# Attention tiles in a pool that closes among the gate tiles, and maxima spread one tile later, in a two-layer decoder trunk

## The chip, the core and the metric

One core of one Trainium2 chip runs the whole program. Its engines are TensorE (PE in the profile; PEld is its weight load), VectorE (DVE), ScalarE (ACT), GpSimd (POOL) and SyncE (SP), whose queue issues the DMAs. Each engine works through its own instructions in the order in which they were queued, and waits on semaphores. The metric is device microseconds of one execution: lower is better. Shown runs of the kernel before have a median of 1673.81 us.

## The reference, cut to what matters

Two post-norm layers over 1024 tokens of 1024 channels. Layer A mixes with dilated sliding-window attention (three groups of keys, merged by their softmax sums), layer B with a sliding window and learned sinks. Both multiply the mixer's output by a SiLU gate before the output projection:

```python
o = einsum('gbsh,gbshd->bshd', softmax(lses), outs)       # layer A: three groups merged
z = h[..., -A_WIDTH:]                                      # gate, from the same input projection
mix = (o * silu(z)) @ w_out
x = layer_norm(ALPHA * x + mix, ln_g[i], ln_b[i])
x = x + sigmoid(x @ ple_w_gate[i]) * (p[i] @ ple_w_proj[i])
```

Everything is float32; the kernel makes it from float16 halves (below).

## The kernel before

**Products.** Every operand of a projection is scaled by a power of two and split into a float16 high part and a low part; a product is three float16 matmuls (high times high, high times low, low times high; L270 to L272). A *tile* of a projection is 128 tokens by 512 output columns: 24 matmuls, with one PSUM buffer of the three that the pool `ps_lin` has, until another engine has read it out.

**Weights.** Weights come in blocks of 1024 rows by 512 columns (`Block`). Each needs its four loads (L102), four reductions of the largest magnitude (L108), the maximum's spreading over all partitions, and four splits on ScalarE and VectorE (L131, L132). The spreading has two halves: `max_diag` makes a diagonal matrix on VectorE (`mdd`, L228), and `max_spread` multiplies it by ones on TensorE (L235), so that VectorE can reduce the result to the scale. All of this is one generator, `weight_steps`, of ten steps for each block. After each tile `prepare(n)` adds n to a credit and takes that many steps: 1.6 for most tiles, 5 for gate tiles of the second half (L934), 2 for output tiles, 3 for tiles of the last product. A step that cannot go on yet (the slot of the block before last is still read, or the pool it needs is not open) yields False and the credit falls to 0. `next_block` takes all steps that are left of a block that is needed now. Two raw buffers, two slots `whl`, and one slot each of `wo` (in the pool `pw`) and `wg` (in the pool of that name) hold the blocks.

**Order.** The program is written out tile by tile; what is written earlier has the higher priority, and a list scheduler, with an estimate of all durations, puts the instructions on the engines' queues in the order in which it finds them ready. So an instruction can be queued well ahead of its place in the program, and the order on each queue is fixed when the program runs.

**Layer A.** 18 blocks of V and of Q and K, eight tiles each. Behind the tiles run the attention *units*: scores (L383), maxima, exponentials, a transposing DMA `pT<-phl` (L402), and values (L414 to L416), queued with a lag. `work_done` counts tiles; `later` and `sub_tick` let units come due by it. The last units of layer A still run beside the first gate tiles. For each 128 tokens and half of the heads, a `merge` joins the three groups (tiles `gt`, loads L745, store L767), one stage for each tile. Then come the gate tiles: 16 of them, eight for each half of the columns (`z_block`, `z_tile`), whose rows `za` (`zb` in layer B) are stored to memory (L725).

**From gate to output projection.** `z_block` does the eight tiles of the first half and one of the second; `drain` then writes out what is left of units and merges, the pool `att` closes, and the pools `tp` (transposed rows) and `pw` (rows, `wo`, and the tables `g_b`, `b_b` of the norm) open over its space, on the other side of the free memory. A tile in a new pool waits until all that lay at its place is done. `mixed` then writes the seven other gate tiles; behind the fifth to the eighth tile of that half stands `rows(n)`: two loads (L894, L895), the product of mixer and gate on GpSimd (L898), the largest sum on ScalarE (L900), a split (L261, L262) and a transposing DMA `ogT<-rhl` (L874). Output tiles need `ogT`; `norm(n)` does two of them, then the norm, with `g_b` at L924. The pool `wg` opens behind the fourth output tile, when the pools below have closed. Layer B goes the same way, with its own pools `kv` and `att2`, and without merges; its units end in a store `ob<-mu` (L860).

## Time and profile before

| | us |
|---|---|
| three runs | 1684.5, 1673.64, 1673.81 |
| median | 1673.81 |
| the profiled execution | 1672.76 |
| its span, first to last instruction | 1670.9 |

The granted clock has a mean of 0.985 over the span; 1.0 stands for 2.4 GHz and 0.5 for 1.2 GHz. Times of rows are microseconds from the span's start. From the trace, the parts of the program lie as follows: gate tiles of layer A up to 1054.6, its output projection from 1064.9 to 1162.4, its last product to 1245.3, layer B's attention to about 1425 with its gate tiles beside and behind it to 1495.4, layer B's output projection to 1583.6.

### The profile page before, as it was taken

How to read it: one execution, taken by the hardware profiler on the slowest of the kernel's cores; microseconds unless marked ns; L12 is line 12 of the kernel's file. 1: busy time of each engine (PE TensorE's matmuls, PEld its weight loads, DVE VectorE, ACT ScalarE, POOL GpSimd, SP SyncE). 2: the span in 40 equal slices, each digit the busy share in tenths (PEclk: the TensorE clock that was granted, in tenths of full speed). 3: DMA queues.
4: the chain of work that ended last, by engine and by line, in shares of the span. 5: the costliest groups of instructions: out<-in, count | busy, mean ns of one | idle time of the engine just before them, and what ended most of it. 6: DMA issues, size and time to landing. Idle time of an engine off the chain costs nothing.

```text
span 1670.9 us, 29003 instructions
## 1 busy us (share of the span) xinstructions
PE 1587.2 (95%) x10579; PEld 879.7 (53%) x10579; DVE 1080.0 (65%) x2617; ACT 922.0 (55%) x2050; POOL 671.6 (40%) x481
## 2 busy tenths in 40 slices
PE   9899999999999889999999997789999999999999
PEld 3455666654555446666545543334456555544444
DVE  6756655655656875456556567788437989777731
ACT  4536755674775377556647844433333888854221
POOL 0205623532554665144235743343323452225441
PEclk9999999999999999999999998899999999999999
DMA  9617765774788777467648885989976798988963
GB/s 364 244 60 171 169 146 133 165 162 112 164 163 208 208 161 160 120 153 158 153 117 176 181 248 192 314 233 237 247 190 138 143 209 176 189 300 218 256 199 111
DMA packets 543791, 311.02 MB, mean 186 GB/s; under 512 B 473120, under 2 KB 494240, under 8 KB 543392
## 3 DMA queue, kind: packets, MB, share of 16 engines
q1 hardware_dynamic: 543648, 309.16, 73.6%
q8 instruction: 83, 1.36, 0.4%
q14 instruction: 60, 0.49, 0.1%
HBM read 137.78 MB, written 54.92 MB: 115 GB/s over the span
## 4 chain that ended last, share of the span: by engine, by line
PE 59%; DVE 14%; DMA 12%; issue 5%; POOL 4%; ACT 3%; SPq 2%; POOLq 0%; DVEq 0%; ACTq 0%
PE lin L270 18%; PE lin L272 18%; PE lin L271 18%; DMA pT<-phl 4%; DVE whl L132 3%; PE s L383 3%; DVE wpm L108 2%; DMA gt<-scr 2%; ACT sm L393 1%; DVE sm L387 1%; PE o L414 1%; PE o L416 1%; PE o L415 1%; POOL hl L356 1%; DMA wraw<-in_wg_dram 1%
## 5 line engine op out<-in xcount | busy, mean ns | idle before, releaser
L270 PE MATMUL lin<-whl,xhl 128*128 128x512 f16 x1280 | 488.9, 382 | 0.0
L271 PE MATMUL lin<-whl,xhl 128*128 128x512 f16 x1280 | 487.7, 381 | 0.0
L272 PE MATMUL lin<-whl,xhl 128*128 128x512 f16 x1280 | 487.5, 381 | 0.0
L399 POOL TENSOR_TENSOR phl<-sm,phl 128x1024 f16<-128x1024 f32 (+1 forms) x88 | 156.5, 1778 | 259.6 <-ACT phl L397 215.7
L349 POOL TENSOR_TENSOR t<-t,t 128x512 f32<-128x512 f32 (+1 forms) x120 | 152.2, 1268 | 232.1 <-DVE t L348 226.1
L272 PEld LDWEIGHTS <-xhl 128*128 128x128 f16 x1280 | 149.3, 117 | 125.8 <-issue 2.9
L270 PEld LDWEIGHTS <-xhl 128*128 128x128 f16 x1280 | 149.2, 117 | 117.4 <-issue 2.6
L108 DVE TENSOR_REDUCE wpm<-wraw 128x1 f32<-128x1024 f32 (+1 forms) x132 | 157.2, 1198 | 82.7 <-DMA wraw<-in_wa_dram 47.4
L271 PEld LDWEIGHTS <-xhl 128*128 128x128 f16 x1280 | 149.9, 117 | 115.2 <-issue 2.3
L393 ACT ACTIVATE sm<-sm,st,cs 128x128 f32<-128x128 f32 (+1 forms) x384 | 203.4, 531 | 3.3 <-ACT st L391 0.4
L356 POOL TENSOR_TENSOR hl<-t,hl 128x512 f16<-128x512 f32 (+1 forms) x120 | 142.7, 1189 | 136.0 <-ACT hl L355 136.0
L387 DVE CUSTOM_DVE_ANT_0 sm<-s,tab 128x256 f32<-128x256 f32 (+1 forms) x512 | 157.0, 359 | 53.7 <-PE s L383 51.9
L132 DVE SCALAR_TENSOR_TENSOR whl<-wraw,s,whl 128x1024 f16<-128x1024 f32 (+1 forms) x116 | 165.0, 1473 | 4.7 <-ACT whl L131 4.6
L345 DVE TENSOR_TENSOR t<-lin,rope 128x512 f32<-128x512 f32 (+1 forms) x120 | 78.9, 658 | 119.3 <-PE lin L272 83.1
L355 ACT ACTIVATE hl<-t 128x512 f16<-128x512 f32 (+1 forms) x120 | 72.1, 601 | 121.0 <-POOL t L349 119.2
L131 ACT ACTIVATE whl<-wraw,s 128x1024 f16<-128x1024 f32 (+1 forms) x116 | 121.9, 1122 | 12.6 <-DVE s L210 6.5
L272 PE MATMUL lin<-whl,x2T 128*128 128x512 f16 (+1 forms) x320 | 115.0, 359 | 0.0
L271 PE MATMUL lin<-whl,x2T 128*128 128x512 f16 (+1 forms) x320 | 115.0, 359 | 0.0
L270 PE MATMUL lin<-whl,x2T 128*128 128x512 f16 (+1 forms) x320 | 114.9, 359 | 0.0
L397 ACT ACTIVATE phl<-sm 128x1024 f16<-128x1024 f32 (+1 forms) x128 | 110.2, 861 | 2.7 <-DMA pT<-phl 1.5
L359 ACT ACTIVATE hl<-hl 128x512 f16<-128x512 f16 (+1 forms) x104 | 63.1, 607 | 59.0 <-POOL hl L356 58.8
L414 PEld LDWEIGHTS <-pT 128*128 128x128 f16 x800 | 72.2, 98 | 34.9 <-DMA pT<-phl 31.1
(190 smaller groups left out, 2901.7 us busy)
## 6 DMA issues: line engine op xcount, KB each, us to landing
wraw<-in_wa_dram SPq DMA_DIRECT2D x56, 512.0 KB, 5.2
scr<-st SPq DMA_DIRECT2D x96, 132.0 KB, 2.4
gt<-scr SPq DMA_DIRECT2D x48, 264.0 KB, 3.3
wraw<-in_wav_dram SPq DMA_DIRECT2D x24, 512.0 KB, 6.1
prh<-pro SPq DMA_DIRECT2D x32, 256.0 KB, 4.5
wraw<-in_wg_dram SPq DMA_DIRECT2D x16, 512.0 KB, 9.0
xg<-y SPq DMA_DIRECT2D x16, 512.0 KB, 3.7
wraw<-in_wb_dram SPq DMA_DIRECT2D x16, 512.0 KB, 6.3
```

The lines of the kernel that those rows point to most:

```text
L108: k.nc.vector.tensor_reduce(pm[:, c:c + 1], self.raw[:, c * q:(c + 1) * q], axis=AX.X, op=ALU.max, apply_absolute_value=True)
L131: nc.scalar.activation(hl[:, 0, sl], self.raw[:, sl], AF.Copy, scale=self.s)
L132: nc.vector.scalar_tensor_tensor(hl[:, 1, sl], self.raw[:, sl], self.s, hl[:, 0, sl], op0=ALU.mult, op1=ALU.subtract)
L270: mm(ps, xh(kt), wh, start=(kt == 0), stop=False)
L271: mm(ps, xh(kt), wl, start=False, stop=False)
L272: mm(ps, xl(kt), wh, start=False, stop=(kt == NK - 1))
L349: nc.gpsimd.tensor_add(t1[:, :nh * HD], t1[:, :nh * HD], t2[:, :nh * HD])
L356: nc.gpsimd.tensor_sub(hl[:, :nh, HD:P], rv, hl[:, :nh, 0:HD])
L387: nc.vector.tensor_tensor_reduce(sm[:, h, :nk], ps[:, i, :nk], mask, 1.0, -3e38, ALU.add, ALU.max, mx[:, h:h + 1])
L393: nc.scalar.activation(sm[:, h, :nk], sm[:, h, :nk], AF.Exp, bias=nbias[:, h:h + 1], scale=cs, accum_out=sums[:, h:h + 1])
L397: nc.scalar.activation(hl[:, 0], sm[:, :, :nk], AF.Copy)
L399: eng.tensor_sub(hl[:, 1], sm[:, :, :nk], hl[:, 0])
```

## The change

The pool `att` no longer holds the tiles of the merges, `st` and `gt`: they get a pool `attm` of their own, below it; the tile `hl` moves from `work` to `att`. The function `drain` is gone. The new `gate_tiles` writes all eight gate tiles of the first half, at three steps each, and as soon as no unit is due, queued or in the pipe, calls `leave`, which closes `att` (in layer B `att2` and `kv`) and opens `tp` and `pw`. `mixed` writes all eight tiles of the second half, at three steps each; merges go on beside them. When merges and gate tiles are written, `gate_pool` closes what is left below and opens the pool `wg`, now ahead of the output projection, and with `g_b` and `b_b` in it. In `Block.maxima` the step that spreads the maximum waits until 0.9 tiles more have been written since the diagonal, unless `next_block` is in a hurry (`rush`). At the start, four of the eleven last products of the per-layer inputs are written ahead of the first block's splits.

```diff
 UNIT_LAG = 1.67
 W_STEPS = 1.6
+SPREAD = 0.9
 W_OP = 2
 N_WAKE = 8
-Z_AHEAD = 1
+W_GATE = 3
...
         diag = k.max_diag(pm)
         yield True
+        at = k.work_done + SPREAD
+        while k.work_done < at and not k.rush:
+            yield False
         e = k.max_spread(diag)
...
-    def drain(self):
-        due, self.due = self.due, []
-        for e in due:
-            e[1]()
-        while self.units or any(self.pipe):
-            self.unit_step()
-        self.merge_every = 1
-        while self.merges or self.merging:
-            self.merge_step()
...
-        hl = w.tile([P, 12, P], F16, tag="hl", name="hl", bufs=3)
+        hl = self.att.tile([P, 12, P], F16, tag="hl", name="hl", bufs=3)
...
+                ple1(4)
                 while not self.blocks[0].done:
                     next(self.steps)
-                ple1(11)
+                ple1(7)
...
+        self.rush = True
         while not b.done:
             assert next(self.steps)
+        self.rush = False
...
         self.merge_every = 1
-        self.z_block(self.invx, lambda n: self.stat_a(0, n))
-        self.drain()
+        self.z_in = self.invx, lambda n: self.stat_a(0, n)
...
-    def z_block(self, invx, stat):
-
-        self.z_stat = stat
+    def z_block(self, half):
+
+        invx, self.z_stat = self.z_in
+        self.w_z = self.next_block()
+        self.cz = self.prod(invx, self.w_z.inv, 0.5, "cz")
+
+    def gate_tiles(self, leave):
+
         self.upt = 2.0
-        for half in range(2):
-            self.w_z = self.next_block()
-            self.cz = self.prod(invx, self.w_z.inv, 0.5, "cz")
-            for n in range(Z_AHEAD if half else NT):
-                self.z_tile(self.work, n, half)
-                self.progress()
-            if half == 0:
-                self.w_z.released = True
+        self.z_block(0)
+        for n in range(NT):
+            self.z_tile(self.work, n, 0)
+            self.progress(W_GATE)
+            if leave and not (self.due or self.units or any(self.pipe)):
+                leave()
+                leave = None
+        assert leave is None
+        self.w_z.released = True
...
-        g_b = pw.tile([P, D], F32, tag="g_b", name="g_b", bufs=1)
-        b_b = pw.tile([P, D], F32, tag="b_b", name="b_b", bufs=1)
-        nc.sync.dma_start(g_b, a["lng"][l].partition_broadcast(P))
-        nc.sync.dma_start(b_b, a["lnb"][l].partition_broadcast(P))
...
+        self.z_block(1)
         done = 0
-        for n in range(Z_AHEAD, NT):
+        for n in range(NT):
             self.z_tile(self.work, n, 1)
             self.tick()
-            self.prepare(5)
+            self.prepare(W_GATE)
             if n >= NT - ROWS_AHEAD:
                 rows(done)
                 done += 1
+        while self.merges or self.merging:
+            self.merge_step()
+        gp = gate_pool()
+        g_b = gp.tile([P, D], F32, tag="g_b", name="g_b", bufs=1)
+        b_b = gp.tile([P, D], F32, tag="b_b", name="b_b", bufs=1)
+        nc.sync.dma_start(g_b, a["lng"][l].partition_broadcast(P))
+        nc.sync.dma_start(b_b, a["lnb"][l].partition_broadcast(P))
         self.w_z.released = True
...
-            if n == 1:
-                wg = gate_pool()
...
-        with tc.tile_pool(name="att", bufs=2) as self.att:
-            self.layer_a()
-        tp, self.tp = opened("tp", 9, side="right")
-        pw, self.pw = opened("pw", 2, side="right")
+        for name in ("work", "attm"):
+            p, pool = opened(name, 2)
+            setattr(self, name, pool)
+            lower.append(p)
+        att, self.att = opened("att", 2)
+        self.layer_a()
+        pools = []
+
+        def row_pools(first, last):
+            for p in first:
+                close(p)
+            for name, bufs in last:
+                p, pool = opened(name, bufs, side="right")
+                setattr(self, name[:2], pool)
+                pools.append(p)
...
+        self.gate_tiles(lambda: row_pools([att], [("tp", 9), ("pw", 2)]))
...
+        self.gate_tiles(lambda: row_pools([att, kv], [("pw2", 2)]))
```

## Rows read from the trace of the kernel before

**Rows 1.** The page's first part: busy time, share, instructions.

```profile
PE 1587.2 (95%) x10579; PEld 879.7 (53%) x10579; DVE 1080.0 (65%) x2617; ACT 922.0 (55%) x2050; POOL 671.6 (40%) x481
```

**Rows 2.** TensorE's longest wait in total: us, times, longest one.

```profile
PE o L414 <- DMA pT<-phl: 23.4, 17, 2.8
```

**Rows 3.** Busy time by stretch: PE, PEld, DVE, ACT, POOL; clock, DMA share, GB/s.

```profile
951.00:1162.40 211.40, 179.98 (x943) 82.66 (x940) 162.73 (x332) 92.23 (x147) 96.23 (x59) 0.94 0.84 240
...
1017.00:1054.60 37.60, 28.85 (x122) 12.26 (x119) 24.80 (x50) 13.52 (x20) 12.45 (x11) 0.86 0.71 255
1054.60:1162.40 107.80, 88.50 (x388) 38.90 (x388) 90.74 (x181) 42.49 (x50) 45.98 (x26) 0.92 0.91 246
1162.40:1245.30 82.90, 82.90 (x386) 37.59 (x384) 36.27 (x46) 25.56 (x30) 23.33 (x18) 1.00 0.88 227
...
1495.40:1583.60 88.20, 84.63 (x385) 38.05 (x386) 67.22 (x128) 35.55 (x38) 38.25 (x22) 0.98 0.92 240
```

**Rows 4.** Timeline of TensorE at single instructions; in brackets the idle time before.

```profile
992.11 0.20 PE L414 MATMUL o<-vh,pT 128*128 128x64 f16 x1 [0.46 <-DMA pT<-phl]
...
1036.16 0.29 PE L235 MATMUL s<-mdd,ones 128*128 128x128 bf16 x1 [8.75 <-DVE mdd L228]
...
1064.86 0.58 PE L270 MATMUL lin<-whl,ogT 128*128 128x512 f16 x1 [10.23 <-ACT whl L131]
...
1498.97 0.26 PE L235 MATMUL s<-mdd,ones 128*128 128x128 bf16 x1 [3.62 <-DVE mdd L228]
```

**Rows 5.** Busy time by stretch around the idle times of layer A.

```profile
1027.40:1036.20 8.80, 0.05 (x2) 0.04 (x2) 8.73 (x20) 1.95 (x3) 3.63 (x3) 0.73 0.35 134
1036.20:1041.70 5.50, 5.50 (x14) 2.02 (x15) 2.58 (x4) 2.66 (x3) 0.00 (x0) 0.50 0.57 191
...
1054.60:1064.90 10.30, 0.07 (x2) 0.07 (x2) 10.23 (x19) 8.51 (x12) 4.86 (x3) 0.70 1.12 339
1064.90:1069.00 4.10, 4.10 (x10) 1.39 (x11) 4.10 (x5) 2.93 (x5) 2.63 (x2) 0.50 1.06 262
...
1114.00:1146.90 32.90, 24.12 (x98) 10.18 (x98) 28.69 (x64) 8.75 (x9) 14.11 (x8) 0.90 0.88 231
```

**Rows 6.** Timeline of the DMA issues on SyncE's queue, layer A.

```profile
1020.19 0.38 SPq L725 DMA_DIRECT2D za<-zu  x1
...
1036.73 0.37 SPq L767 DMA_DIRECT2D oa<-gt  x1
1039.01 0.33 SPq L884 DMA_DIRECT2D g_b<-in_lng_dram  x1
...
1040.81 0.61 SPq L895 DMA_DIRECT2D og<-za  x1
...
1056.45 6.11 SPq L874 DMA_TRANSPOSE ogT<-rhl  x1
```

**Rows 7.** VectorE's groups of instructions from 951 to 1162.4: count, busy, mean ns.

```profile
L132 DVE SCALAR_TENSOR_TENSOR whl<-wraw,s,whl 128x1024 f16<-128x1024 f32 (+1 forms) x13 | 23.4, 1824 | 0.4 <-ACT whl L131 0.4
...
L262 DVE SCALAR_TENSOR_TENSOR rhl<-og,rs,rhl 128x1024 f16<-128x1024 f32 x8 | 11.1, 1385 | 2.1 <-ACT rhl L261 1.9 <-issue 0.2
...
L132 DVE SCALAR_TENSOR_TENSOR wo<-wraw,s,wo 128x1024 f16<-128x1024 f32 x4 | 5.0, 1280 | 2.9 <-ACT wo L131 2.9
```

**Rows 8.** The same timeline of SyncE's queue in layer B.

```profile
1471.92 0.38 SPq L860 DMA_DIRECT2D ob<-mu  x1
1474.11 0.33 SPq L884 DMA_DIRECT2D g_b<-in_lng_dram  x1
...
1475.44 0.43 SPq L895 DMA_DIRECT2D og<-zb  x1
```

**Rows 9.** Second block of weights: TensorE's spread.

```profile
90.86 0.22 PE L235 MATMUL s<-mdd,ones 128*128 128x128 bf16 x1
```

**Rows 10.** Second block of weights: VectorE's splits.

```profile
93.15 4.88 DVE L132 SCALAR_TENSOR_TENSOR whl<-wraw,s,whl 128x1024 f16<-128x1024 f32 x4 [0.48 <-ACT whl L131]
```

**Rows 11.** Products of the token tiles by weights: duration ns, first and last start.

```profile
L270 PE MATMUL lin<-whl,xhl x1280: 378/379/634, 64.0 to 1053.8; 128*128 128x512 f16 x183
```

More of the change, by code (lines that the diff above doesn't have):

```diff
@@ L949, in mixed, with gate @@
                 done += 1
-            if n == 1:
-                wg = gate_pool()
         for b in w_o:
             b.released = True
-        return xgT, xg_dr, wg
-    def gate(self, l, xgT, xg_dr, last):
+        return xgT, xg_dr, gp
+    def gate(self, l, xgT, xg_dr, gp, last):
         nc, a, pw = self.nc, self.a, self.pw
@@ L974, in gate @@
                 self.lin(ps, w_g[hf], *self.stat_t(xgT, n), c0 % 512, w)
-                t = pw.tile([P, 512], F32, tag=("g_b", "b_b")[hf], name="gth", bufs=1)[:, :w]
+                t = gp.tile([P, 512], F32, tag=("g_b", "b_b")[hf], name="gth", bufs=1)[:, :w]
                 nc.scalar.activation(t, ps, AF.Tanh, scale=cg[hf])
@@ L1066, in build @@
         lower.append(work)
-        with tc.tile_pool(name="kv", bufs=1) as self.kv, tc.tile_pool(name="att2", bufs=2) as self.att:
-            self.layer_b(x2T, self.x2_s[1])
-        pw, self.pw = opened("pw2", 2, side="right")
-        xgT, xg_dr, wg = self.mixed(1, lambda n: x2_dr[n], lambda: gate_pool("wg2"))
-        self.gate(1, xgT, xg_dr, True)
-        close(wg)
-        close(pw)
-        close(tp)
+        kv, self.kv = opened("kv", 1)
+        att, self.att = opened("att2", 2)
+        self.layer_b(x2T, self.x2_s[1])
+        self.gate_tiles(lambda: row_pools([att, kv], [("pw2", 2)]))
+        xgT, xg_dr, gp = self.mixed(1, lambda n: x2_dr[n], lambda: gate_pool("wg2"))
+        self.gate(1, xgT, xg_dr, gp, True)
+        while pools:
+            close(pools.pop())
 @with_exitstack
```

21 lines of the change are left out of this document (10 added, 11 removed).

## Prediction, made before the change was run

> **What bounds the kernel now.** The page comes first: TensorE is busy for 95% of the span, VectorE for 65% [rows 1]. So every us that can be won is one of the 83.7 in which TensorE is idle (1670.9 less 1587.2), or one in which it runs at half its clock. The second view is TensorE's waits. The largest in total is for transposed exponentials, 23.4 us in 17 pieces of at most 2.8 [rows 2]: thin, spread over both layers, and nothing of it is touched here. The third view, the same idle time at single instructions, shows where the thick ones lie: 8.75 us before the spread of a maximum among the gate tiles of layer A, 10.23 us before the first output tile, 3.62 us before a spread at the same place in layer B [rows 4]. The fourth view, busy time by stretch, gives the whole loss. The last product of layer A, 16 tiles, takes 82.9 us with nothing idle [rows 3], so a tile is 5.18 us. By that measure the output projection of layer A (16 tiles, also 82.9) loses heavily, and layer B's, 88.2 us, loses 5.3 [rows 3].
>
> Read with the waits, the stretches also show who is late. While TensorE stands still for 8.75 us, VectorE is busy for 8.73 of 8.80; in the second stop for 10.23 of 10.30; and from 1114 to 1146.9 for 28.69 of 32.90 [rows 5]. But just before, from 1017 to 1054.6, it has only 24.80 of 37.60 [rows 3]. VectorE is thus not short of time over the whole stage (162.73 of 211.40 [rows 3]); its work comes too late. After each long stop the granted clock is 0.50, the 1.2 GHz level, for 5.5 us and for 4.1 us [rows 5], in which half the pace is lost: 2.75 and 2.05 us.
>
> **The change part by part.** Sums are against the profiled execution, 1672.76 us (span 1670.9 and 1.86 around it), 1.05 below the median of 1673.81.
>
> *The spread among the gate tiles, layer A.* It belongs to the first block of the last product. Before, five steps for each gate tile put its reductions, its diagonal and its spread behind the fifth tile of the second half, spread right behind diagonal. At three steps, with one tile between, the count gives the diagonal behind the eighth tile and the spread behind the first output tile. That is four tiles later on TensorE, 20.7 us, while the diagonal was 8.75 late. The wait goes wholly, and so does the slow clock behind it: 8.75 + 2.75 = **11.5 us**. The spread of the second output block moves from behind the third gate tile to behind the fifth; it did not wait before. With this, gate tiles end at 1027.4 + 3 x 5.18 = 1042.9, not 1054.6.
>
> *The first output tile.* What is late next is its transposed row. Before, that chain (load, GpSimd product, sum, split, transpose) ran from its second load at 1040.81 to the first output matmul at 1064.86 [rows 4, 6], 24.05 us. It could not begin earlier, since the row tiles lie over `att`, whose last user was a merge: its store is issued at 1036.73, and the tables and rows follow on SyncE's queue from 1039.01 [rows 6]. In the new order `att` holds units only, whose last values run at 992.11 [rows 4]. So the start is set by the data: the first gate row of the second half, stored no later than the issue at 1020.19 [rows 6] says, or at worst by the place in the program, the fifth gate tile at 1027.4. Ends: 1020.2 + 24.05 = 1044.2 (1.3 us after the gate tiles) and 1027.4 + 24.05 = 1051.5 (8.6 after). I take 1047: layer B shows that the queue runs rows ahead of their place, with the load at 1475.44 [rows 8] although the fifth gate tile ends three tiles before 1495.4, at 1479.9. That leaves a wait of 4 us and 1 us of slow clock out of 10.23 + 2.05: **7.3 us** won, bounds 1.7 and 12.3.
>
> *The output projection of layer A.* From 1114 to 1146.9, 98 matmuls take 32.9 us [rows 5]; at 24 in 5.18 they need 21.2: a loss of 11.7, with VectorE busy for 87%. Three of the eight row splits (1385 ns each [rows 7]) leave the stage, some 4.2 us, as their rows now come before it. But VectorE's 90.74 us there [rows 3] only fall to about 86, against 82.9 of TensorE. So part of the loss stays; I take **4.7** of 11.7, bounds 0 and 11.7.
>
> *Output weights.* The second block's four splits (5.0 us on VectorE [rows 7]) have their slot in the same pool `pw`; they now lie behind the fifth gate tile, in the stretch where VectorE had 12.8 us free. Nothing on the path; if that cover is gone, 5 us.
>
> *Layer B.* No merges here, but its stores `ob<-mu` come from `att2`: the last is issued at 1471.92, and the tables and rows follow from 1474.11 [rows 8], as before, since units end where they did. Rows start no earlier. Of the 5.3 us the spread's part can go, but the first row is nearly as late as the spread was. I take **2**, bounds 0 and 5.3.
>
> *The norm's tables.* `g_b` and `b_b` are now loaded when the last gate tile is done, and SyncE's queue stands until then with whatever is queued behind them: transposes and rows. They are needed after two output tiles, 10.4 us later; before, `g_b` was issued at 1039.01 [rows 6], ahead of the rows. In layer B they lie over the gate rows' tiles and wait for those stores too. Cover: VectorE can be two output tiles behind before the three PSUM buffers are full. I take −0.5, bounds −4 and 0.
>
> *Spreads elsewhere.* A block takes ten steps, 6.25 tiles at 1.6; one tile more, and the credit lost at False, make about 7.5 of its eight. The tightest case is the second block: first tile at 64.0 [rows 11], so its end is near 106; spread at 90.86 [rows 9], splits until 98.03 [rows 10]. A tile later they end at 103.2, still 3 us early. Once the slots bind, splits start when a slot comes free, as before. 0. That the queues are laid out anew can move the thin waits, 23.4 us [rows 2], either way; I allow 5 us on both sides.
>
> *At the start*, four products ahead of the splits leave TensorE's own order as it is, and no matmul waits for those readouts: 0.
>
> Sum: 11.5 + 7.3 + 4.7 + 2 − 0.5 = 25, less 1 for a spread elsewhere that now waits: 24. 1672.76 − 24 = 1648.8; with the 1.05 to the median, **1650**.
>
> **Rivals.**
> 1. *Rows start at their place* (1027.4) and the chain keeps its 24 us. Then the first output tile starts 8.6 us after the gate tiles, with 2 of slow clock; it saves 1.7, and the later stage and layer B keep their losses: 11.5 + 1.7 = 13.2, so 1661. For it: SyncE's queue is one, and the tables stand in it. Against it: rows 8.
> 2. *VectorE is the bound of the stage.* Its share from 951 to 1162.4 is 0.770 [rows 3]. If that is all it reaches, the same work takes the same 211 us, wherever TensorE waits: 1668 to 1676, say 1672. For it: both stops are filled with VectorE work [rows 5]. It would be worse where GpSimd works beside it: the splits into `whl` take 1824 ns in the mean, those into `wo` 1280 [rows 7]. Against it: 12.8 us free just before. The Trainium skill, "SBUF — State Buffer", section "Who interferes with whom", says that a VectorE instruction with two SBUF inputs contends with a GpSimd instruction that reads SBUF; rows moved beside gate tiles would then slow the splits there, which speaks against this change. By it the four `wo` splits would take 1824 ns, 2.2 us more, and this rival 1674; the two means agree with it, though no row here shows the cause.
> 3. *Slower: spreads stand in the output projection.* By the count three lie there in layer A (both blocks of the last product, of which the first is new there, and layer B's first) and two in layer B, where VectorE is at 84% (90.74 of 107.80 [rows 3]). TensorE takes them in order, so a diagonal that comes more than a tile (5.18 us) after its place stops it, as at 1036.16. At 11.5 each, three give 34.5 back: 1650 + 34.5 = 1684; from two on nothing is won. Against it: the stage had spreads before, and both waits for a diagonal [rows 4] lie ahead of its first output tile's end.
> 4. *All of it*: 11.5 + 12.3 + 11.7 + 5.3 = 41: 1633.
>
> **How the numbers follow.** Forecast (1640 to 1658) 0.48, rival 1 0.20, rival 2 0.12, rival 3 0.08, all of it 0.12. A measurement of this kernel tells about 1% (16.7 us, 1657.1) from no change. Faster by more: 0.48 + 0.12 + a fifth of rival 1 = 0.64. Within 1%: the rest of rival 1 and rival 2, 0.28. Slower: 0.08. The range reaches from all of it to rival 2's value, 1633 to 1674, and leaves out rival 3 and part of rival 2.
>
> **What would show it.** No wait over 2 us at L235 in layer A's gate tiles; `ot` and `og` loads before 1030; first output matmul by 1050 with an idle time under 6 us before it; `wo` splits near 1030; from there to the end of the output projection under 90 us. Wrong: the first output matmul still more than 8 us behind the last gate tile (rival 1); new waits for `mdd` among output tiles (rival 3); tables that land after the norm's first use; waits for `whl` in the first blocks.

## The result, and the profile after

The changed kernel takes 1701.9 us (median of four runs, 1697.97 to 1704.09); the kernel before took 1676.5 beside it (four runs). The ratio is 1.0141, with an interval from 1.0098 to 1.0184: slower by 1.4%, where 1.4% faster was forecast. The profiled execution has 1697.97 us and a span of 1696.1, 25.2 more than before.

The page's first part of the changed kernel, to hold against [rows 1]:

```profile
PE 1593.5 (94%) x10579; PEld 881.1 (52%) x10579; DVE 1098.9 (65%) x2617; ACT 921.7 (54%) x2050; POOL 681.9 (40%) x481
```

The instructions are the same in number. TensorE is busy for 6.3 us more and idle for 18.9 more. Its waits in the changed kernel (us in total, times, longest), the first row to hold against [rows 2]:

```profile
PE o L409 <- DMA pT<-phl: 38.3, 22, 4.4
PE lin L275 <- DMA ogT<-rhl: 14.8, 4, 8.5
PE o L409 <- DVE mu L860: 8.0, 4, 3.7
PE lin L275 <- ACT zu L715: 7.8, 6, 2.9
...
PE lin L275 <- DVE t L343: 3.1, 1, 3.1
```

Busy time by stretch in the changed kernel, columns as in [rows 3]: layer A from gate tiles to output projection, the second gate half, the output projection, the last product, layer B from its second query block to its last unit, and layer B's first output tile with its output projection.

```profile
963.80:1166.80 203.00, 178.81 (x958) 82.42 (x957) 163.62 (x328) 91.00 (x146) 92.81 (x58) 0.97 0.88 248
1014.40:1064.60 50.20, 43.78 (x194) 19.23 (x193) 37.38 (x70) 23.44 (x35) 25.22 (x19) 0.97 0.77 251
1064.60:1166.80 102.20, 87.94 (x388) 38.54 (x388) 89.72 (x178) 39.20 (x44) 39.96 (x24) 0.97 0.91 254
1166.80:1250.80 84.00, 83.01 (x385) 37.55 (x384) 36.59 (x46) 26.29 (x31) 24.37 (x18) 1.00 0.89 227
...
1328.30:1491.40 163.10, 147.78 (x1459) 87.18 (x1457) 134.58 (x373) 119.59 (x304) 51.08 (x31) 0.96 0.85 176
...
1513.10:1608.80 95.70, 85.22 (x388) 38.03 (x387) 76.16 (x139) 36.49 (x42) 39.60 (x22) 0.96 0.93 243
```

The same stretch of layer B in the kernel before, from its second query block to its last unit:

```profile
1320.30:1471.90 151.60, 141.92 (x1451) 84.64 (x1449) 130.97 (x373) 119.86 (x304) 50.98 (x31) 0.99 0.90 188
```

Cut at the first matmuls of each stage, the difference of 25.2 us lies so:

| stretch | before | after | difference |
|---|---|---|---|
| start and layer A's 18 attention blocks | 949.0 | 961.8 | +12.8 |
| layer A, first gate half | 52.3 | 52.6 | +0.3 |
| layer A, second gate half to first output matmul | 63.6 | 50.3 | -13.3 |
| layer A, output projection | 97.6 | 102.2 | +4.6 |
| layer A, last product | 82.9 | 84.0 | +1.1 |
| layer B up to its first output matmul | 253.6 | 270.8 | +17.2 |
| layer B, output projection and last product | 171.9 | 174.4 | +2.5 |

So the gain that was argued came, in its place: TensorE no longer waits for a diagonal among the gate tiles of layer A, and its first output tile does not wait for a row. More than twice as much (12.8 and 19.7) was lost where the forecast put nothing or a gain: among the attention blocks of layer A and in all of layer B. TensorE at the places in question, in the changed kernel:

```profile
929.86 0.20 PE L409 MATMUL o<-vh,pT 128*128 128x64 f16 x1 [2.55 <-DMA pT<-phl]
...
954.18 0.20 PE L409 MATMUL o<-vh,pT 128*128 128x64 f16 x1 [1.94 <-DMA pT<-phl]
...
1057.24 0.38 PE L275 MATMUL lin<-whl,xhl 128*128 128x512 f16 x1 [2.90 <-ACT zu L715]
...
1064.62 0.38 PE L275 MATMUL lin<-whl,ogT 128*128 128x512 f16 x1 [0.35 <-ACT zu L715]
...
1267.25 0.27 PE L275 MATMUL lin<-whl,x2T 128*128 128x256 f16 x1 [3.10 <-DVE t L343]
...
1521.67 0.61 PE L275 MATMUL lin<-whl,ogT 128*128 128x512 f16 x1 [8.48 <-DMA ogT<-rhl]
```

**What VectorE does ahead of the second of them.** Its timeline in the changed kernel, around the reductions of the first output block, and later at layer B's splits into `wo`:

```profile
917.76 1.22 DVE L109 TENSOR_REDUCE wpm<-wraw 128x1 f32<-128x1024 f32 x1 [1.51 <-DMA wraw<-in_ao_dram]
...
925.67 1.22 DVE L109 TENSOR_REDUCE wpm<-wraw 128x1 f32<-128x1024 f32 x1 [4.72 <-DMA wraw<-in_ao_dram]
926.81 0.42 DVE L382 CUSTOM_DVE_ANT_0 sm<-s,tab 128x256 f32<-128x256 f32 x1
...
937.17 1.22 DVE L109 TENSOR_REDUCE wpm<-wraw 128x1 f32<-128x1024 f32 x1 [5.74 <-DMA wraw<-in_ao_dram]
...
939.20 0.68 DVE L394 TENSOR_TENSOR phl<-sm,phl 128x512 f16<-128x512 f32 x1
...
1500.37 8.93 DVE L136 SCALAR_TENSOR_TENSOR wo<-wraw,s,wo 128x1024 f16<-128x1024 f32 x4
```

SyncE's queue in the changed kernel: the four loads of that block, and the end of layer B's attention.

```profile
913.05 0.39 SPq L103 DMA_DIRECT2D wraw<-in_ao_dram  x1
913.54 3.92 SPq L397 DMA_TRANSPOSE pT<-phl  x1
...
920.04 1.05 SPq L103 DMA_DIRECT2D wraw<-in_ao_dram  x2
921.20 6.10 SPq L397 DMA_TRANSPOSE pT<-phl  x1
...
932.17 0.87 SPq L103 DMA_DIRECT2D wraw<-in_ao_dram  x1
...
1491.39 0.32 SPq L862 DMA_DIRECT2D ob<-mu  x1
1493.35 0.32 SPq L892 DMA_DIRECT2D ot<-ob  x1
```

And the same place in the kernel before, VectorE and SyncE:

```profile
906.81 3.77 DVE L108 TENSOR_REDUCE wpm<-wraw 128x1 f32<-128x1024 f32 x3 [1.01 <-DMA wraw<-in_ao_dram]
```

```profile
902.12 1.76 SPq L102 DMA_DIRECT2D wraw<-in_ao_dram  x4
```

A reduction waits for the load of its own block, and masks and subtractions of the softmax stand behind it on VectorE. Before, the four loads were issued in one go and three reductions ran through after a wait of 1.01 us; in the changed kernel the loads stand between transposes that wait themselves, and VectorE stops for 4.72 and 5.74 us. The wait of 1.94 us at 954.18 can be followed back to the second of these stops. VectorE's product for the rotation (`t`, L343) stands behind the reduction; GpSimd waits for it, ScalarE for GpSimd, and the exponentials behind that on ScalarE for their turn, so that GpSimd's subtraction `phl`, from which the transposition is made, starts at 947.66:

```profile
941.16 1.27 POOL L344 TENSOR_TENSOR t<-t,t 128x512 f32<-128x512 f32 x1 [3.67 <-DVE t L343]
942.46 0.63 ACT L350 ACTIVATE hl<-t 128x512 f16<-128x512 f32 x1 [3.94 <-POOL t L344]
947.66 2.13 POOL L394 TENSOR_TENSOR phl<-sm,phl 128x1024 f16<-128x1024 f32 x1 [3.33 <-ACT phl L392]
```

The wait of 2.55 us at 929.86 does not go back to a stop: its transposition follows a subtraction that GpSimd began at 921.60, before the stop of 4.72 us was over. For the other waits this is not shown.

That a reduction meets its own load at all is not in the written order: there, the loads of a block come ten steps before its reductions. It is in the built order. The program's list for VectorE in the changed kernel, with buffer numbers (13617, 14047 and 14963 are layer B's two gate halves and its first output block; three lines out of many):

```
L136 SCALAR_TENSOR_TENSOR whl_14690<-wraw_13617,s123_14575,whl_14690 128x1024 x3
L109 TENSOR_REDUCE wpm_15982<-wraw_14963 128x1
L136 SCALAR_TENSOR_TENSOR whl_15807<-wraw_14047,s129_15499,whl_15807 128x1024 x3
```

The reductions of the third block stand behind the splits of the first, whose raw buffer the third is loaded into, and ahead of the splits of the second: the scheduler has taken them forward by a block, to the point at which its estimate has them ready. The list of the kernel before has them at the same place.

### The profile page after: what moved, and what is told of

Read it like the earlier page. It is cut to its first block, busy times and chain, and to the rows that moved or that the text cites. A ratio compares the mean times of both kernels' runs of the same rounds, so it can differ in the third digit from the quotient of the medians.

```text
span 1696.1 us, 28996 instructions
## 1 busy us (share of the span) xinstructions
PE 1593.5 (94%) x10579; PEld 881.1 (52%) x10579; DVE 1098.9 (65%) x2617; ACT 921.7 (54%) x2050; POOL 681.9 (40%) x481
## 4 chain that ended last, share of the span: by engine, by line
PE 36%; DVE 11%; DMA 9%; ACT 4%; issue 4%; POOL 2%; SPq 1%; DVEq 0%; ACTq 0%; POOLq 0%
PE lin L275 11%; PE lin L276 11%; PE lin L277 11%; DMA pT<-phl 2%; ACT sm L388 2%; PE s L378 2%; DVE sm L382 1%; DMA og<-za 1%; DVE whl L136 1%; DVE wpm L109 1%; DMA wraw<-in_bo_dram 1%; POOL og L896 1%; DMA ogT<-rhl 1%; DVE rhl L267 1%; DMA gt<-scr 1%
## 5 line engine op out<-in xcount | busy, mean ns | idle before, releaser
L344 POOL TENSOR_TENSOR t<-t,t 128x512 f32<-128x512 f32 (+1 forms) x120 | 157.3, 1311 | 264.2 <-DVE t L343 238.5
L136 DVE SCALAR_TENSOR_TENSOR whl<-wraw,s,whl 128x1024 f16<-128x1024 f32 (+1 forms) x116 | 164.3, 1461 | 13.2 <-ACT whl L135 13.1
L275 PE MATMUL lin<-whl,x2T 128*128 128x512 f16 (+1 forms) x320 | 116.2, 363 | 3.1 <-DVE t L343 3.1
L276 PE MATMUL lin<-whl,x2T 128*128 128x512 f16 (+1 forms) x320 | 116.3, 363 | 0.0
L277 PE MATMUL lin<-whl,x2T 128*128 128x512 f16 (+1 forms) x320 | 116.1, 363 | 0.0
```

The source lines that it names most:

```text
L136: nc.vector.scalar_tensor_tensor(hl[:, 1, sl], self.raw[:, sl], self.s, hl[:, 0, sl], op0=ALU.mult, op1=ALU.subtract)
L275: mm(ps, xh(kt), wh, start=(kt == 0), stop=False)
L276: mm(ps, xh(kt), wl, start=False, stop=False)
L277: mm(ps, xl(kt), wh, start=False, stop=(kt == NK - 1))
L344: nc.gpsimd.tensor_add(t1[:, :nh * HD], t1[:, :nh * HD], t2[:, :nh * HD])
```

## The experiments

Every kernel was run in three rounds beside the kernel before (`e17` in five). This table has what the text below reads from them: the ratio to before with its interval; where layer A's attention ends; the time from there to layer A's last product; layer B from its start to the store of its last unit (`ob<-mu`); how many gate tiles TensorE has left behind that unit; and the time from that store to the first output matmul. All but the ratio come from one profiled execution each; where two kernels have the same program up to a point, these differ by up to some 4 us.

| kernel | ratio | A's attention ends | gates and output, A | B to last unit | gate tiles behind it | store to first output |
|---|---|---|---|---|---|---|
| before | 1 | 949.0 | 213.4 | 226.5 | 4.6 | 27.1 |
| changed | 1.0141 [1.0098, 1.0184] | 961.8 | 205.0 | 240.6 | 4.3 | 30.3 |
| e1 spread | 1.0079 [1.0058, 1.0101] | 960.6 | 209.2 | 237.6 | 3.7 | 26.3 |
| e2 pools | 1.0093 [1.0072, 1.0114] | 955.6 | 212.3 | 241.6 | 4.3 | 26.9 |
| e3 start | 1.0003 [0.9986, 1.0020] | 949.9 | 213.7 | 227.1 | 4.6 | 27.2 |
| e4 both | 1.0153 [1.0137, 1.0169] | 962.7 | 206.0 | 240.3 | 4.3 | 30.6 |
| e5 before, tied | 1.0085 [1.0058, 1.0112] | 948.0 | 214.2 | 239.8 | 1.2 | 28.5 |
| e6 after, tied | 1.0018 [1.0006, 1.0031] | 944.3 | 210.5 | 242.3 | 1.1 | 27.4 |
| e7 hl in work | 1.0103 [1.0076, 1.0130] | 960.5 | 207.4 | 237.5 | 3.7 | 27.4 |
| e8 gate steps | 1.0102 [1.0079, 1.0124] | 960.9 | 205.0 | 240.8 | 4.4 | 26.0 |
| e9 after, held | 1.0076 [1.0053, 1.0100] | 942.9 | 215.2 | 245.4 | 1.1 | 27.3 |
| e10 before, held | 1.0080 [1.0051, 1.0109] | 949.5 | 207.6 | 241.0 | 1.1 | 28.4 |
| e11 mended | 1.0073 [1.0051, 1.0095] | 946.8 | 213.6 | 243.6 | 1.0 | 30.4 |
| e12 mended, early | 1.0059 [1.0043, 1.0076] | 950.1 | 204.8 | 244.7 | 0.9 | 29.8 |
| e13 the same, pinned | 1.0101 [1.0073, 1.0129] | 948.6 | 211.5 | 242.4 | 1.2 | 29.8 |
| e14 after, held, pinned | 1.0094 [1.0067, 1.0120] | 944.3 | 215.7 | 241.0 | 1.1 | 24.2 |
| e15 before, held, pinned | 1.0100 [1.0068, 1.0132] | 952.6 | 211.3 | 243.6 | 1.1 | 26.9 |
| e16 after, pinned | 1.0170 [1.0143, 1.0197] | 958.2 | 207.6 | 241.4 | 4.3 | 30.6 |
| e17 deferred | 1.0079 [1.0058, 1.0101] | 949.0 | 204.4 | 243.0 | 0.9 | 23.6 |
| e18 products on VectorE | 1.0201 [1.0181, 1.0220] | 960.4 | 213.8 | 243.0 | 4.3 | 28.0 |

What the expectations call layer B's two query blocks is, read exactly, the second query block and the first gate half, beside which the last units run.

### Which part costs: e1 to e4

`e1` puts only the later spread into the kernel before:

```diff
+        at = k.work_done + SPREAD
+        while k.work_done < at and not k.rush:
+            yield False
```

> The kernel before with only the later spread (one tile between a block's diagonal and its spread, unless the block is needed at once). Theory S (the later spread re-lays the work on weights among the attention blocks of both layers, and that is what costs): A's attention and layer B's k, v and q blocks lose together 20 to 26 us as in the changed kernel; the wait of 8.75 us among the gate tiles of A shrinks to under 4; in all 12 to 22 us slower than before. Theory P (the pools and the gate tiles' new order cost): the attention parts stay within 3 us of before, and the time is 0 to 8 us below before. Theory O (any re-laying of the queues moves the thin waits by some 10 us, without a rule): the change is neither, and does not add up with that of the pools alone.

Slower by 0.8%, 11.5 us, where S had 12 to 22. Layer A's attention lost 11.6 us and, with the 11.1 us of layer B, the sum is in S's 20 to 26; the wait for the diagonal in the gate tiles went; layer B's last unit came 11.1 us later.

`e2` is the changed kernel without it and with the start as before:

```diff
-SPREAD = 0.9
+SPREAD = -1.0
```

> The changed kernel without the later spread and with the start as before: pools and gate tiles alone. Theory S: the gain of the gate tiles in full, 8 to 13 us at that place, attention parts as before, so 8 to 16 us faster than before. Theory P: attention of A 8 to 13 us longer, layer B 15 to 20 us longer, in all 15 to 25 us slower. Theory O: some 10 us of thin waits more or less, at other places than in the changed kernel.

Slower by 0.9%, 14.8 us. So S is not the whole: layer A's attention lost 6.6 us (P had 8 to 13), and layer B's last unit came 15.1 later, the lower end of what P had said.

`e3` has the start alone:

```diff
+                ple1(4)
                 while not self.blocks[0].done:
                     next(self.steps)
-                ple1(11)
+                ple1(7)
```

> The kernel before with only four products of the start ahead of the first block's splits. Theories S and P: within 2 us of before, everywhere. Theory O: A's attention differs by more than 3 us from before although nothing in it was edited.

No change, and every column is within 1 us of before. Laying the queues anew at the start does not by itself move the thin waits: O, as a mere lottery, falls for an edit that leaves the blocks' steps where they were.

`e4` is the changed kernel with the start as before (`ple1(11)`).

> The changed kernel with the start as before: later spread and pools together. Theories S and P: within 3 us of the changed kernel, 22 to 29 us above before. Theory O: more than 5 us from the changed kernel, either way.

As the changed kernel. The ratios of `e1` and `e2` make 1.017 together, `e4` has 1.015: both parts cost, about half each, and in both it is the same two places.

### The reductions behind their own load: e5, e6, e9, e10

The reductions of a block are held behind the spread of the block ahead by one shared buffer:

```diff
-        pm = k.small.tile([P, 4], F32, tag="wpm", name="wpm")
+        pm = k.small.tile([P, 5], F32, tag="wpm", name="wpm", bufs=1)
...
-        e = k.max_spread(diag)
+        e = k.max_spread(diag, pm[:, 4:5])
```

Here `max_spread` writes its result into the fifth column, so the buffer is free only when the scale has been made from it.

> The kernel before, with the reductions of a block held behind the spread of the block ahead of it: both share the only buffer of wpm, and no instruction is added. In the order that was built for VectorE, a block's four reductions stand right behind the load of that same block, a whole block earlier than written, and VectorE stands until the load lands. Theory Q (these stops delay the masks of the scores and so the transposed exponentials): the waits for pT shrink by a third to a half, 5 to 15 us faster than before. Theory O (any re-laying moves the thin waits without a rule): within 5 us of before, the waits for pT at other places.

> The changed kernel with the same hold. Theory Q: its loss in the attention parts (some 13 us in A, some 9 in B without k and v) mostly goes: 15 to 25 us faster than the changed kernel, 0 to 8 us faster than before; the wait at B's first rotated tiles (3 us) stays. Theory O: less than 8 us faster than the changed kernel, the attention of A still some 10 us longer than before.

`e6` answers to Q against the changed kernel: 1678.9 us, 23 below it (20.6 by the ratios to before), and layer A's attention ends at 944.3, 17.5 earlier. It is still 3.0 us above before, where Q had 0 to 8 below. But `e5`, which Q had 5 to 15 us faster, is slower by 0.9%. The view of the tile `wpm` names what VectorE sat idle for ahead of the reductions, in us and times. Changed kernel:

```profile
  DMA wraw<-in_wa_dram: 41.0, 26
  DMA wraw<-in_ao_dram: 12.0, 3
```

and `e6`, where no load is left in the list:

```profile
  PE s L240: 11.3, 8
```

TensorE's waits in `e6`: those for `pT` fall to less than half, and a new one takes the top.

```profile
PE s L240 <- DVE mdd L233: 22.9, 2, 22.2
PE o L410 <- DMA pT<-phl: 16.4, 13, 3.6
```

That new wait, 22 us before layer B's first output tile, is in `e5` too. `e9` and `e10` hold only the blocks of the attention, of the gate halves and the first output block of each layer (`self.blocks[:21] + self.blocks[25:30]`).

> The changed kernel with the hold on attention's blocks, the gate halves and each layer's first output block alone; the tails' other blocks keep two buffers and the built order. Theory Q (reductions that stand behind their own load cost the attention parts): attention of A 10 to 18 us shorter than in the changed kernel, layer B's two query blocks 14 to 18 us shorter, as with the hold everywhere, and no wait of 22 us before layer B's first output tile: 1662 to 1673 in all, at or below before. Theory O: attention falls back to within 5 us of the changed kernel's, since the order is laid anew once more.

> The kernel before with the same hold on the same blocks. Theory Q: the query blocks of layer B some 4 us shorter, attention of A within 5 us of before, the tails as before: 1664 to 1675. With the run above it gives what the change is worth where reductions do not stand behind their own load: by the tails' own times (gate tiles to last product, 4 to 14 us) the changed order should win. Theory O: 1675 to 1690, as with the hold everywhere.

The wait of 22 us stayed in both, and both miss Q's totals: 1689.4 us (1662 to 1673) and 1687.5 (1664 to 1675). With this hold the change itself is worth nothing (`e9`, with the change, 1.0076; `e10`, without it, 1.0080); with the hold on all blocks it is worth 0.7% (`e6` 1.0018, `e5` 1.0085). In layer A, Q holds: over all kernels here its attention ends at

| | spread as before | spread later |
|---|---|---|
| reductions as built | 949.0, 949.9 (955.6 with the new pools) | 958.2 to 962.7 (seven kernels) |
| reductions held | 948.0 to 952.6 (six kernels) | 942.9 to 946.8 (four kernels) |

As built, the later spread costs 11.6 us (`e1`), or 7.1 with the new pools (`e4` against `e2`). Held, the attention ends some 5 us earlier with it, but that is no gain: the first gate half then takes 59.1 to 60.6 us instead of 50.6 to 51.5, and the second begins at 1002.0 to 1006.2, against 998.9 to 1004.1 with the spread as before. As built, it begins at 1013.1 to 1016.2 with the later spread, and at 1001.3 and 1004.7 without (1009.5 with the new pools). So what the later spread costs layer A depends on where the reductions stand. That they wait is not enough: before, VectorE waits for loads there just as long (62.8 us up to the end of layer A's attention in either kernel), and holding them wins nothing. What is left is what stands behind them, which the step that yields False moves; that was followed for the one wait above and is argued for the rest.

### Two smaller terms: e7 and e8

`e7` puts layer B's `hl` back into the work pool.

```diff
-        hl = self.att.tile([P, 12, P], F16, tag="hl", name="hl", bufs=3)
+        hl = (self.hlp or self.att).tile([P, 12, P], F16, tag="hl", name="hl", bufs=3)
```

> The changed kernel with layer B's rotated tiles (hl) back in the work pool. Theory H (in the attention pool they lie over the row halves rhl of layer A's last rows, and wait for their last transposition): layer B's k and v block takes 21 us again, not 24.3, with no 3.1 us wait in it; the rest as in the changed kernel, so 3 to 5 us faster than it. Rival: the block keeps its 24 us, since what it waits for is the last transposed row itself.

H holds: the k and v block takes 21.0 us, not 24.3, and is 21.0 in every kernel with this edit. The whole is some 6 us below the changed kernel by the ratios, a little more than H's 3 to 5: the time from store to first output is 2.9 us shorter too, and no run here shows why. In the changed kernel ScalarE shows what it waited for, the last transposition out of `rhl`, over which `hl` now lies:

```profile
1265.77 0.51 ACT L350 ACTIVATE hl<-t 128x128 f16<-128x128 f32 x2 [3.98 <-DMA x2T<-rhl]
```

`e8` gives the gate halves their old steps.

```diff
-            self.progress(W_GATE)
+            self.progress()
...
-            self.prepare(W_GATE)
+            self.prepare(5)
```

> The changed kernel with the steps on weights as before among the gate tiles: 1.6 a tile in the first half, 5 in the second, not 3 and 3. Theory G (in layer B three steps a tile put the splits into wo beside GpSimd's products, where each took 2.23 us instead of 1.22, and the first output tile waits 8.5 us): layer B's step from gate tiles to output shrinks from 8.5 to some 4 us, while in A the splits come later and 2 to 6 us of the 13 won there are lost; in all within 4 us of the changed kernel. Rival: the place of the rows alone sets both, and nothing moves.

Layer B's first output matmul comes 3.8 us behind the last gate tile instead of 8.5, and in layer A 5.2 us of the second gate half are lost and 6.5 of the output projection won. All in all some 6.5 us below the changed kernel by the ratios to before (8.6 by the medians, 1693.3 and 1701.9), more than the 4 expected, though the two intervals overlap; G has the direction and the places.

### Where the held kernels lose it again: e11 to e17

`e11` joins the hold, `e7` and `e8`; `e12` is the same without the later spread.

> The changed kernel with three things at once: the same hold, layer B's rotated tiles in the work pool, and 1.6 and 5 steps a tile in the gate halves. If the parts measured so far add up: attention as with the hold, k and v 21 us, gate tiles and output projections some 4 us below the changed kernel's: 1650 to 1662, 1% faster than before. Theory O: above 1668.

> The same without the later spread. Theory S2 (with the hold in place the later spread costs the attention nothing): attention within 4 us of the run above, and the gate tiles of A wait for a diagonal again, 3 to 8 us slower in all. Rival: the later spread still costs the first blocks of A some 6 us (blocks 0 to 2 took 145.2 us with it and 139.6 without), and the time is 2 to 8 us below the run above.

Neither adds up: both are slower than before by 0.6 to 0.7%, with 26 us between layer B's last gate tile and first output matmul. S2 has it half: the later spread costs layer A's attention nothing under the hold, and `e12` waits 6.3 us for a diagonal among the gate tiles, but its total is 1.0 us below that of `e11`, not 3 to 8 above. The spread of the last product's second block stands, in TensorE's built order, ahead of layer B's first output tile, a hundred instructions before its written place, and the profile put the wait down to it. So the tails' order was pinned, with this at both calls of `mixed`:

```diff
+        with tc.manual_schedule(engines={mybir.EngineType.PE}):
```

> The mended kernel without the later spread, with TensorE's instructions in their written order from the second gate half to the end of the output projection, in both layers. Theory T: layer B's step to the first output tile shrinks from 26.3 to 3 to 7 us, the attention stays: 1660 to 1670. Theory R: the wait turns into one for the transposed row, 15 us or more: above 1675.

> The changed kernel with the hold, layer B's rotated tiles in the work pool, and TensorE's written order in the tails; 3 steps a tile and the later spread stay. Theory T: query blocks of layer B 60 to 65 us each, k and v 21, the step to layer B's first output tile 4 to 9 us: 1660 to 1672. Theory R: above 1676.

> The kernel before with the same hold and the same written order. Theory T: the 23 us at layer B's first output tile fall to 3 to 7 us: 1662 to 1672; the difference to the run above is what the changed tails are worth, 0 to 8 us in either direction. Theory R: above 1676.

> The changed kernel with TensorE's written order in the tails alone. Both theories: nothing stands ahead of its place there, so within 5 us of the changed kernel, query blocks 70 us each.

T falls, and R has it: `e13` to `e15` take 1692.8 to 1694.4 us. TensorE at layer B's first output tile, in `e12`, and then in `e13`, where the spread stands in its written place:

```profile
1510.35 0.29 PE L242 MATMUL s<-mdd,ones 128*128 128x128 bf16 x1 [24.37 <-DVE mdd L235]
```

```profile
1515.35 0.61 PE L278 MATMUL lin<-whl,ogT 128*128 128x512 f16 x1 [23.83 <-DMA ogT<-rhl]
```

The wait has the same length under another name: the transposed row was as late as the diagonal. Pinning alone (`e16`) gains nothing either. The written order also costs elsewhere: from layer B's first output matmul to the end, `e14`, `e15` and `e16` take 182.8, 179.0 and 180.9 us, where `e9`, `e10` and the changed kernel take 173.0, 174.3 and 174.4 (`e13` takes 172.4, `e12` 173.1). `e17` takes `e13` and writes the spread of the last product's first block, and so its splits, behind the first output tile:

```diff
+        while self in k.after_rows and not k.rows_out:
+            yield False
         e = k.max_spread(diag, pm[:, 4:5] if held else None)
```

> The mended and pinned kernel (hold, layer B's rotated tiles in the work pool, steps of the gate halves as before, no later spread elsewhere), with one thing more: the spread of the last product's first block, and so its four splits, is written behind the first output tile, in both layers. Theory V (these splits stand ahead of the first rows in VectorE's queue): layer B's step to the first output tile falls from 23.8 to 4 to 8 us, the wait of 20 us for a diagonal among layer A's second gate half goes, the output projections are up to 6 us longer: 1652 to 1666, faster than before by 0.6 to 1.4%. Theory R2 (the rows are late for their own sake: stores, loads, products): 15 us or more stay in layer B, 1675 to 1685.

V falls in layer B (the row still comes 20 us late) and holds in layer A, where the wait of 20.3 us for a diagonal went and the second gate half took 50.4 us, not 64.1, at 6.7 us more in the output projection. What is left is R2, and the last two columns of the table say what it is. SyncE's queue in `e17`, and TensorE:

```profile
1480.18 0.38 SPq L868 DMA_DIRECT2D ob<-mu  x1
1482.33 0.32 SPq L898 DMA_DIRECT2D ot<-ob  x1
```

```profile
1503.79 0.61 PE L280 MATMUL lin<-whl,ogT 128*128 128x512 f16 x1 [20.20 <-DMA ogT<-rhl]
```

In all twenty kernels the first output matmul of layer B comes 23.6 to 30.6 us after the store of the last attention unit; the loads of the rows follow that store by 2 to 3 us in every one. Whether TensorE stands still meanwhile is set by the gate tiles that it has left: 4.6 before (24 us of work, a wait of 3.6), 0.9 to 1.2 with the hold. With the hold TensorE takes 3.2 to 3.5 more gate tiles ahead of the last units. In `e9`, the stretch behind the last unit and the stretch up to the first output tile:

```profile
1485.80:1491.40 5.60, 5.60 (x28) 2.45 (x25) 3.08 (x4) 4.35 (x5) 0.00 (x0) 1.00 0.41 146
1491.40:1513.60 22.20, 0.13 (x3) 0.04 (x2) 21.31 (x37) 11.49 (x16) 12.16 (x8) 0.59 0.96 338
```

These tiles filled the waits for `pT` between the last units, and then were missing behind them. So the shorter first gate half of the held kernels is no gain: what sets layer B is when its last unit is done, and that is 226.5 us after its start before, 227.1 in `e3`, and 237.5 to 245.4 in all others.

### VectorE beside GpSimd: e18

```diff
-                nc.gpsimd.tensor_mul(og[:, sl], og[:, sl], ot[:, sl])
+                nc.vector.tensor_mul(og[:, sl], og[:, sl], ot[:, sl])
```

> The changed kernel with the rows' products (og times ot) on VectorE, not GpSimd. Theory G2 (splits are slowed by GpSimd's products beside them): layer B's four splits into wo take 1.28 us each, not 2.23, and the wait of 8.5 us before the first output tile shrinks to 3 to 6 us; the output projections may lose 0 to 8 us, since VectorE takes 10.9 us more in each. Rival (the splits are slow for another reason, a transfer or ScalarE beside them): still above 2 us each.

The whole is slower, 1.0201, since VectorE takes over work in both output projections. But G2 holds: layer B's four splits into `wo`, at 2.23 us each in the changed kernel (8.93 for four, above; one takes 2.29 from its start to its end), take 1.28 us here, and the first output tile waits 6.3 us instead of 8.5, a little outside the 3 to 6 expected. VectorE in `e18`, the first of them:

```profile
1512.13 1.28 DVE L136 SCALAR_TENSOR_TENSOR wo<-wraw,s,wo 128x1024 f16<-128x1024 f32 x1
```

GpSimd in the changed kernel over the same splits; the products run from 1498.63 to 1510.42, the splits from 1500.37 to 1509.30:

```profile
1498.63 11.79 POOL L896 TENSOR_TENSOR og<-og,ot 128x512 f32<-128x512 f32 x6 [29.23 <-DMA og<-zb]
```

The Trainium skill, "SBUF — State Buffer", section "Who interferes with whom", has it that a VectorE instruction with two SBUF inputs contends with a GpSimd instruction that reads SBUF; both runs agree with it.

## Why the prediction was wrong

**The step that failed is "Spreads elsewhere", with "units end where they did" in "Layer B".** The first counted in tiles, in the written order, that a spread a tile later still comes in time for its splits, and it does: no wait for splits came up in the first blocks. But the step asked only whether the moved instruction itself comes too late. It did not ask what the move does to VectorE's queue, whose order is built from estimates. There the reductions of each block stand a block ahead, behind the load of their own block, and a stop there holds up what stands behind it. Forecast 0 (with 1 us taken off in the sum), measured +12.8 us in layer A, 6.5 of it in the last of the 18 blocks, where the stops of 4.72 and 5.74 us are. That the place of the reductions decides is shown by the 2 by 2 table, in which the loss goes with the hold; that each block's loss runs through a stop is shown for the wait at 954.18 alone.

"Layer B" took 2 us of gain and measured a loss of 17.2 up to the first output matmul and 19.7 in all. Of the 17.2, 14.1 are that the last unit is done later. It can be taken apart by rows: 3.3 from `hl` over `rhl` (shown, `e7`), less 0.7 in the first query block; from the second query block to the last unit, 163.1 us instead of 151.6, which is 11.5: 5.6 of idle time (163.10 less 147.78 against 151.60 less 141.92) and 5.9 of busy time, of which eight matmuls more make some 1.7 and the slower clock (0.96 against 0.99) the rest. The remaining 3.1 are the chain from the store to the output, 30.3 instead of 27.1, with the splits beside GpSimd in it (8.93 us for four, 4.9 before). Why these thin waits came at both parts of the change alike is not settled: with the reductions held, the idle time there falls to some 6 us (`e9`), so they are the likely cause, but the last unit comes no earlier, since TensorE then takes gate tiles first. No run here separates the two.

**"The spread among gate tiles" and "the first output tile"** forecast 11.5 and 7.3, together 18.8; measured 13.3. Both waits of [rows 4] are gone, and the first output matmul waits 0.35. The row came about when it was forecast. Its first load, `ot`, went out at 1013.87, but the chain was counted from the second, `og`, and that one is issued at 1039.15, when a gate row's store has landed: 24.8 us behind the start of the half, at the late end of what was taken (1020.2 and 1027.4 are 18.9 and 26.1 behind it). Its transposition landed at 1059.65, 45.3 us behind the start, where 1047 is 45.7. SyncE in the changed kernel, the store and the load:

```profile
1032.27 0.38 SPq L722 DMA_DIRECT2D za<-zu  x1
...
1039.15 0.33 SPq L893 DMA_DIRECT2D og<-za  x1
```

What is missing is a wait that the forecast did not have: the gate tiles did not run through in 41.6 us but wait three times for ScalarE to read them out, 6.1 us of the 7.8 above (the other three such waits are at output tiles). Ahead of the first, of 1.29 us at 1036.52, ScalarE stood 5.85 us for a merge, which now goes on beside these tiles. Ahead of the two others it takes the row's sum of magnitudes (L898), which waits for GpSimd's products. ScalarE ahead of the longest one, in the changed kernel:

```profile
1054.89 1.06 ACT L898 ACTIVATE ot<-og 128x1024 f32<-128x1024 f32 x1 [4.54 <-POOL og L896]
...
1055.95 0.67 ACT L713 ACTIVATE zt<-lin,cz 128x512 f32<-128x512 f32 x1
1056.52 0.68 ACT L715 ACTIVATE zu<-lin,cz 128x512 f32<-128x512 f32 x1
```

The prediction named SyncE's queue and VectorE's as those that rows are moved past, and left out ScalarE's.

**"The output projection of A"** had its sign wrong: 4.7 won was taken, bounds 0 and 11.7, and 4.6 were lost. Its own sum had VectorE at 86 us against 82.9 of TensorE; measured are 89.72 from the first output matmul on, where the kernel before has 80.51 (90.74 counted from its last gate tile [rows 3]). The row splits that were to leave the stage did not: six of eight start behind the first output matmul, as before. With the old steps among the gate tiles (`e8`) it takes 95.7 us, so three steps a tile push work on weights into it.

**What was right or cost nothing.** The start is worth nothing (`e3`). The tables land 6 us ahead of the norm's first use of `g_b` at 1087.64. The splits into `wo` of layer A take 1.27 us each, as in [rows 7], though at 1059 and not near 1030.

**Rivals.** Rival 1 is nearest for this stage: it had 13.2 us won up to the first output matmul, against 13.3 measured, and its start of the rows, their place in the program, is 1.3 us behind where the load was issued. But that is luck in part: the row was there 5.0 us before the first output matmul, and what held TensorE was the reading of the gate tiles. Rival 2 (VectorE bounds the stage) does not fit: VectorE's share from the first gate half to the last product is 163.62 of 203.00, 0.806 against 0.770 before, where rival 2 had it stay. Rival 3 did not come: no spread stops TensorE among output tiles. The whole was none of the four: all of them looked at the stage that was edited.

**The allowance.** For queues laid out anew 5 us were set on either side, on 23.4 us of waits for `pT` [rows 2]. These waits grew by 14.9 alone; of the eight over 2 us, three (at 555.12, 1356.01 and 1416.50) were followed by matmuls of some 630 ns instead of 379, the 1.2 GHz level. A term without a mechanism was bounded by a feeling, not by a row. A row that bears on it is VectorE's idle time ahead of the reductions, 82.7 us over the whole kernel before. Its sum is no bound, as it is 83.0 in the changed kernel, but it says that much work stands behind loads.

## What to carry to other kernels

When a scheduler builds the queues, an edit has two places: where it is written, and where each engine's built order puts it; look in the trace for instructions of an in-order engine that wait for a load with urgent work behind them, since an edit that shifts loads or steps can be paid there, as layer A's attention paid it here. Attribute a wait by taking it away, not by its label: the wait of 22 us was named after a diagonal, and after a transposed row when the diagonal was moved, while its length was set by a chain that began at the last attention unit and by the filler left beside it. Work that fills a wait early is missing later: in `e10`, 3.5 more gate tiles ahead of the last units came with 6.9 us less from layer B's start to its second gate half, and with 22.7 us more from there to the first output matmul than before.

Of the eighteen only `e3`, the start alone, is level with the kernel before; the best of the others, `e6`, is 1.0018 [1.0006, 1.0031] times before. No run beat the kernel before. The parts that were best apart (layer A's attention to 942.9, gate tiles and output in 204.4, the last product 82.9, and layer B in 425.5 as before) make a span of 1655.7, but no kernel here had them together, and the first two are not independent (where the attention ends earliest, the first gate half is 8 to 10 us longer); whether one can is open.

## What the runs showed of the hardware that had not been expected

- A split of 1024 columns on VectorE takes 1.28 us by itself (`e18`) and 2.29 beside GpSimd's products (changed kernel); in the same stretch GpSimd's six products take 11.79 us, 1.97 each; before, six of them took 8.46 us in the stretch from 1471.3 to 1495.4.
- Short waits can cost more than their length: from layer B's second query block to its last unit, 5.6 us more of idle time came with some 4 us lost at a lower mean clock (0.96 against 0.99; an estimate from the busy time, less eight matmuls). Not each does: of the eight waits for `pT` over 2 us in the changed kernel, three were followed by matmuls at the 1.2 GHz level.
